# Filter norms: square roots by logarithm, exponential and one Newton step; spectra added up in DRAM

## The chip, the cores and the metric

The kernel runs on one core of a Trainium2 chip. Its parts that matter here are TensorE (matrix products into PSUM), VectorE and GpSimd (elementwise work), ScalarE (elementwise work, and functions looked up in tables that have to be loaded), SyncE (which only issues DMAs here) and 16 DMA engines between on-chip memory (SBUF) and DRAM. Each engine runs its own list of instructions in order, and waits at an instruction until what it needs is there. DMAs are issued from SyncE's queue, from ScalarE's and from GpSimd's; those from GpSimd can add to what stands at the destination. The metric is the device time of one execution, in microseconds.

## The reference

One layer of a hybrid encoder works on a sequence of 1024 steps with 1024 channels: RMS norm, one input projection, a state-space branch (S5), a Hyena branch, a gated merge, an output projection and a final norm. The change touches how the Hyena filters' spectra are made:

```
h = sin(freq * (feats @ w1 + b1));  h = sin(freq * (h @ w2 + b2))
h = (h @ w3) * (exp(-t * |decay|) + 0.05)          # 1024 steps, 2 orders x 2 directions x 1024 channels
k = concat([h_fwd, 0, flip(h_bwd[1:])])            # length 2048
k = k * rsqrt(sum(k * k, axis=0) + 1e-6)           # a norm per channel
kf = rfft(k)                                       # used in both Hyena steps: irfft(rfft(z) * kf)
```

The input's RMS norm, `x * rsqrt(mean(x * x) + 1e-6) * w`, uses the same root function.

## The kernel before

The work goes through stages: the filters (with the input's norm spread among them), then the input projections interleaved with the S5 branch, then the two Hyena convolutions, the branch projections, the merge and the output.

**Filters.** They are made in eight units of 256 channels: two orders times four quarters. `filter_time` makes a unit's filters in eight tiles of 128 time steps. For each tile TensorE multiplies (tile g), ScalarE takes the exponential of the decay (e), VectorE multiplies the two (into e again), ScalarE squares it (sq), and VectorE or GpSimd forms sum and difference of the two directions (so, or ss and sd). For the odd time steps ScalarE and VectorE split these into a high and a low part (sh, sl). GpSimd adds up the squares (acc). `filter_norm` sums acc over the partitions on TensorE (q), takes the root, and corrects one row of the filters with it (transposes into q, then ss). `filter_freq` makes the spectrum: products of the odd time steps (po, 24 matmuls for each of four blocks of frequencies jj) and of the even ones (pe). `join` copies half of pe to SBUF (eo), forms the sum and difference of the even halves (ke), and adds and subtracts po. The four combinations (ko) are stored in the DRAM tensor kspec, one store of 512 KB for each block.

While unit u's time tiles are made, the products of unit u-1 are issued between them; the loop in `filters` sets which step comes with which. A scheduler in the framework then orders each engine's instructions, within the constraints that the code gives (`issue_after`, `high_priority`).

**The root.** `rsqrt` starts from a bit trick and takes three Newton steps, column by column, all on VectorE: for a norm of two columns two operations and twelve small ones, for the input's norm of eight columns two and 48.

**Projections.** Each takes a weight block of 512 KB. `prefetch` loads it (wraw), ScalarE casts it to its high part (whi) and writes the negative of that to wlo, and a DMA from GpSimd's queue adds wraw to wlo. A projection is 48 matmuls; the last 16 read wlo. Three buffers of wraw and two of whi and wlo set how far this runs ahead. `stage_constants` copies the constants of the Hyena stages within DRAM during the first S5 block. kspec is read (tile kt) by `forward`, in the Hyena stages after the S5 branch.

The lines that the steps below name: L119 to L126 the root, L336 the exponential e, L338 its product, L371 the sums q, L383 the transposes, L404 po, L421 eo, L425 and L426 ke, L429 and L430 ko, L508 to L512 the weights' loading, L556 the projections.

Of the kernel before, what the change touches and what calls it, by code (L numbers as in the profile page):

```python
# [9 lines left out]
F = mybir.dt.float32  # L10
# [9 lines left out]
NCH = 256  # L20
# [80 lines left out]
class Trunk:  # L101
# [13 lines left out]
    def rsqrt(self, pool, out, v, n):  # L115

        V = self.nc.vector
        h = pool.tile([128, n], F, name="rsq_h", tag="rsq_h")
        V.tensor_scalar(out=out.bitcast(I32), in0=v.bitcast(I32), scalar1=-0.5, scalar2=float(0x5F3759DF),  # L119
                        op0=ALU.mult, op1=ALU.add)  # L120
        V.tensor_scalar(out=v, in0=v, scalar1=-0.5, scalar2=None, op0=ALU.mult)
        for _ in range(3):
            for c in range(n):
                y, z = out[:, c:c + 1], h[:, c:c + 1]
                V.scalar_tensor_tensor(out=z, in0=y, scalar=v[:, c:c + 1], in1=y, op0=ALU.mult, op1=ALU.mult)  # L125
                V.scalar_tensor_tensor(out=y, in0=z, scalar=1.5, in1=y, op0=ALU.add, op1=ALU.mult)  # L126

# [13 lines left out]
    def setup(self, ctx):  # L141
        tc, nc, I = self.tc, self.nc, self.I
        self.keep = ctx.enter_context(tc.tile_pool(reuse_waits="tile", name="keep", bufs=1))
        self.dram = ctx.enter_context(tc.tile_pool(name="scratch", bufs=1, space=DRAM))
        k = self.keep
        self.ident = k.tile([128, 128], F, name="ident")
        self.ones = k.tile([128, 1], F, name="ones")
        nc.vector.memset(self.ones, 1.0)
        self.par = k.tile([128, 128], F, name="par")
        self.nrm = k.tile([128, 16], F, name="nrm")  # L150
        self.p_norm = self.par[:, 0:8]
        self.p_cw = self.par[:, 8:80].rearrange("p (j c) -> p j c", j=3)
        self.p_cb = self.par[:, 80:104]
        self.p_d = self.par[:, 104:120]
        self.p_bglu = self.par[:, 120:124]
        self.kspec = self.dram.tile([2, 4, 4, 128, 4 * NCH], F, name="kspec")

    def params(self):
# [84 lines left out]
    def filters(self, ctx, top):  # L243
# [13 lines left out]
        for u in range(len(units) + 1):  # L257
# [18 lines left out]
            if u == len(units):  # L276
                self.filter_norm(*units[u - 1], sds)
                c2.close()
                self.weight_pools(top)
                self.proj_pools(top)  # L280
                self.prefetch()
            for i in range(12):
                next(t, None)
                if i == 0 and u < len(units):
                    with tc.high_priority(offset=40):
                        self.filter_norm(*units[u - 1], sds)
                if i >= f0:
                    with tc.issue_after(self.f_g.ins):
                        next(f)
                if i % 3 == 0:  # L290
                    with tc.issue_after(self.f_sq.ins):
                        next(x, None)
                if i == 6 and u + 1 < len(units):
                    self.filter_load(*units[u + 1])()
# [28 lines left out]
    def filter_time(self, o, cq, sds, pool):  # L323
# [6 lines left out]
        for n, tt in enumerate((4, 5, 6, 7, 0, 1, 2, 3)):  # L330
# [32 lines left out]
            yield  # L363

    def filter_norm(self, o, cq, sds):

# [9 lines left out]
        nrm = self.nrm[:, col:col + 2]  # L376
        self.rsqrt(up, nrm, qs, 2)
        r = q[:, NCH:]
        for ct in range(2):
# [8 lines left out]
    def filter_freq(self, o, cq, sds):  # L388
# [7 lines left out]
        def odd(jj):  # L396

            po = pk.tile([128, 2, NCH], F, name="po", bufs=2)
            for part in range(2):
                blocks = (((0, 1, 2, 3), (4, 5, 6, 7)), ((4, 5, 8, 9), (10, 11, 2, 3)))[jj // 2][part]  # L400
                n = 0
                for i, b in enumerate(blocks):
                    for a, d in ((0, 0), (0, 1), (1, 0)):
                        nc.tensor.matmul(out=po[:, part], lhsT=fo[a][:, 12 * (jj % 2) + b], rhs=sd[4 + i][d][:, part],  # L404
                                         start=n == 0 and part == 0, stop=n == 11 and part == 1)
                        n += 1
                yield po

# [8 lines left out]

        def join(j, po):
            pe = even(8 * j + 4, (2, 3))
# [3 lines left out]
            pe = even(8 * j, (0, 1))  # L423
            ke = wp.tile([128, 2, 2, NCH], F, name="ke", bufs=1)
            nc.vector.tensor_tensor(out=ke[:, 0], in0=pe, in1=eo, op=ALU.add)  # L425
            nc.vector.tensor_tensor(out=ke[:, 1], in0=pe, in1=eo, op=ALU.subtract)  # L426
            for jj in (j, j + 2):
                ko = wp.tile([128, 4, NCH], F, name="ko")
                nc.vector.tensor_tensor(out=ko[:, 0:2], in0=ke[:, jj // 2], in1=po[jj], op=ALU.add)  # L429
                nc.vector.tensor_tensor(out=ko[:, 2:4], in0=ke[:, jj // 2], in1=po[jj], op=ALU.subtract)  # L430
                nc.sync.dma_start(out=self.kspec[o, cq, jj], in_=ko.rearrange("p a c -> p (a c)"))

        for j in range(2):
            po = {}
            for jj in (j, j + 2):
                for po[jj] in odd(jj):
                    yield
            yield from join(j, po)
            yield
# [50 lines left out]
    def weight_pools(self, ctx):  # L490
# [8 lines left out]
        self.order += [("w_branch_hy", c, 8) for c in range(8)]  # L499
        self.weights, self.w_more = [], []  # L500

    def prefetch(self):

        nc = self.nc
        while (len(self.weights) < 2 or self.w_more) and self.order:
# [5 lines left out]
            nc.scalar.activation(out=lo, in_=hi, func=AF.Copy, scale=-1.0)  # L511
            nc.gpsimd.dma_start(out=lo, in_=raw, accum_op=ALU.add)  # L512
            self.weights.append((nxt, hi, lo))
# [956 lines left out]
    def run(self):  # L1470
        tc = self.tc
        with ExitStack() as ctx:
# [5 lines left out]
            with ExitStack() as cf:  # L1478
# [3 lines left out]
                with tc.tile_pool(reuse_waits="tile", name="f_mlp", bufs=1, side="right") as mp, \  # L1482
                        tc.tile_pool(reuse_waits="tile", name="f_mlp_ps", bufs=2, space=PSUM, side="right") as mpp:
                    self.filter_mlp(cp, mp, mpp)
                self.filters(cf, ctx)
            self.conv_weights()
            with ExitStack() as c3:
# [52 lines left out]
```

## Time and profile before

Three runs took 1414.94, 1415.73 and 1419.7 us; the median is 1415.73 us. The profiled execution took 1413.96 us, and its span, from the first instruction to the last, is 1412.2 us.

| engine | busy us | share of the span | instructions |
|---|---|---|---|
| TensorE, matmuls | 1346.7 | 95% | 7219 |
| VectorE | 1014.1 | 72% | 1934 |
| ScalarE | 515.1 | 36% | 737 |
| GpSimd | 416.6 | 29% | 343 |

These shares are means over stages with different limits. The page's picture of the span in 40 slices shows VectorE nearly full in the first six (the filters) and TensorE nearly full from the seventh on. A wait is charged to the releaser that came last, and idle time of an engine costs nothing unless something late follows from it. In the rows below, PE is TensorE, PEld its weight loads, DVE VectorE, ACT ScalarE, POOL GpSimd and SP SyncE; a q behind a name is the queue of that engine.

### The profile page before, as it was taken

How to read it: one execution, taken by the hardware profiler on the slowest of the kernel's cores; microseconds unless marked ns; L12 is line 12 of the kernel's file. 1: busy time of each engine (PE TensorE's matmuls, PEld its weight loads, DVE VectorE, ACT ScalarE, POOL GpSimd, SP SyncE). 2: the span in 40 equal slices, each digit the busy share in tenths (PEclk: the TensorE clock that was granted, in tenths of full speed). 3: DMA queues.
4: the chain of work that ended last, by engine and by line, in shares of the span. 5: the costliest groups of instructions: out<-in, count | busy, mean ns of one | idle time of the engine just before them, and what ended most of it. 6: DMA issues, size and time to landing. Idle time of an engine off the chain costs nothing.

```text
span 1412.2 us, 19536 instructions
## 1 busy us (share of the span) xinstructions
PE 1346.7 (95%) x7219; PEld 1135.9 (80%) x7219; DVE 1014.1 (72%) x1934; ACT 515.1 (36%) x737; POOL 416.6 (29%) x343
## 2 busy tenths in 40 slices
PE   5888899999999999999999997999999999999997
PEld 3777798888888887788788885998888889878886
DVE  7999997699599887414479997663899836843632
ACT  5576664222332333333322222443222234422422
POOL 3766675000000000223112213743013223322322
PEclk9999999999999999999999998999999999999999
DMA  8222224865695554566985588769888988755431
GB/s 278 94 78 75 77 100 146 200 173 137 164 301 132 124 124 103 134 173 155 307 244 173 172 241 264 216 179 315 258 268 268 292 247 245 220 161 134 139 112 64
DMA packets 188556, 257.24 MB, mean 182 GB/s; under 512 B 23069, under 2 KB 144153, under 8 KB 185724
## 3 DMA queue, kind: packets, MB, share of 16 engines
q1 hardware_dynamic: 148492, 151.32, 34.0%
q0 software_dynamic: 12608, 43.79, 15.6%
q10 hardware_dynamic: 27360, 60.88, 12.0%
q8 instruction: 57, 0.93, 0.3%
q14 instruction: 39, 0.32, 0.1%
HBM read 147.49 MB, written 76.82 MB: 159 GB/s over the span
## 4 chain that ended last, share of the span: by engine, by line
PE 72%; DVE 18%; DMA 5%; issue 3%; ACT 1%; POOL 1%; SPq 0%; ACTq 0%; DVEq 0%; POOLq 0%
PE pps L556 43%; PE ops L1441 6%; PE iv L643 5%; PE po L404 4%; PE fwo L695 3%; DMA zc<-c_zc_lo_d 2%; PE pe L414 2%; PE pps L536 2%; DVE rsq_h L125 2%; DVE e L338 1%; PE fwe L695 1%; DMA d_y<-x 1%; DVE st L1274 1%; PE zt L680 1%; DVE st L1272 1%
## 5 line engine op out<-in xcount | busy, mean ns | idle before, releaser
L512 POOL DMA_DIRECT2D wlo<-wraw x76 | 66.3, 872 | 673.3 <-ACT wlo L511 530.2
L556 PE MATMUL pps<-xh,whi 128*128 128x512 f32 x848 | 214.2, 400 | 3.2 <-DVE cv L581 3.2
L556 PE MATMUL pps<-xl,whi 128*128 128x512 f32 x848 | 212.3, 397 | 0.0
L556 PE MATMUL pps<-xh,wlo 128*128 128x512 f32 x848 | 210.2, 396 | 0.0
L556 PEld LDWEIGHTS pps<-xh,whi 128*128 128x128 f32 x848 | 158.0, 189 | 39.5 <-ACT wlo L511 3.6
L556 PEld LDWEIGHTS pps<-xh,wlo 128*128 128x128 f32 x848 | 157.9, 188 | 36.8
L556 PEld LDWEIGHTS pps<-xl,whi 128*128 128x128 f32 x848 | 157.3, 188 | 36.3 <-issue 0.2
L510 ACT CAST whi<-wraw 128x1024 fp32r<-128x1024 f32 (+1 forms) x76 | 74.7, 982 | 285.7 <-PE pps L556 254.9
L404 PE MATMUL po<-sh,fo 128*128 128x256 f32 x512 | 101.1, 292 | 6.0 <-DVE sh L111 5.1
L643 PE MATMUL iv<-ic,y 128*128 128x256 f32 (+1 forms) x752 | 97.2, 287 | 5.5 <-POOL y L113 3.1
L643 PEld LDWEIGHTS iv<-ic,y 128*128 128x128 f32 x752 | 95.4, 194 | 8.1 <-POOL y L113 4.0
L404 PEld LDWEIGHTS po<-sh,fo 128*128 128x128 f32 x512 | 84.0, 197 | 8.3 <-DVE sh L111 6.1
L357 POOL TENSOR_TENSOR acc<-acc,sq 128x512 f32<-128x512 f32 x56 | 75.9, 1356 | 24.5 <-ACT sq L342 23.0
L511 ACT ACTIVATE wlo<-whi 128x1024 fp32r<-128x1024 f32 (+1 forms) x76 | 74.9, 985 | 20.7 <-PE pps L556 20.6
L113 DVE TENSOR_TENSOR y<-yraw,y 128x512 fp32r<-128x512 f32 x60 | 55.0, 938 | 28.2 <-ACT y L109 28.2
L404 PE MATMUL po<-sl,fo 128*128 128x256 f32 x256 | 74.2, 290 | 1.0 <-DVE sl L113 1.0
L579 DVE SCALAR_TENSOR_TENSOR cv<-pps,cw,cv 128x1023 f32<-128x1023 f32 x24 | 30.7, 1281 | 59.5 <-ACT cv L578 59.5
L109 ACT CAST y<-yraw 128x512 fp32r<-128x512 f32 x64 | 39.0, 619 | 55.9 <-DMA yraw<-d_y 27.4
L404 PEld LDWEIGHTS po<-sl,fo 128*128 128x128 f32 x256 | 50.4, 197 | 2.2 <-DVE sl L113 1.3
L578 ACT ACTIVATE cv<-pps,cb,cw 128x1024 f32<-128x1024 f32 x24 | 29.0, 1208 | 62.1 <-PE pps L556 43.9
L333 PE MATMUL g<-w3h,ha 128*128 128x512 f32 x64 | 33.3, 520 | 18.6 <-DVE e L338 17.6
L695 PE MATMUL fwo<-z,zc 128*128 128x256 f32 x384 | 49.9, 283 | 0.0
(447 smaller groups left out, 2788.7 us busy)
## 6 DMA issues: line engine op xcount, KB each, us to landing
wlo<-wraw POOLq DMA_DIRECT2D x64, 512.0 KB, 5.7
wraw<-w_in SPq DMA_DIRECT2D x56, 512.0 KB, 5.2
kspec<-ko SPq DMA_DIRECT2D x32, 512.0 KB, 3.6
kt<-kspec SPq DMA_DIRECT2D x32, 512.0 KB, 5.1
yraw<-d_y SPq DMA_DIRECT2D x64, 256.0 KB, 5.3
d_y<-x ACTq DMA_DIRECT2D x28, 512.0 KB, 5.5
d_m<-cv ACTq DMA_DIRECT2D x16, 512.0 KB, 2.6
d_z<-z ACTq DMA_DIRECT2D x8, 1024.0 KB, 5.5
```

What stands on the lines that cost most here:

```text
L109: nc.scalar.copy(out=hi, in_=src)
L113: e.tensor_tensor(out=lo, in0=src, in1=hi, op=ALU.subtract)
L333: nc.tensor.matmul(out=ps, lhsT=ha[:, tsl], rhs=w3h, start=True, stop=False)
L357: nc.gpsimd.tensor_tensor(out=acc, in0=acc, in1=sq, op=ALU.add)
L404: nc.tensor.matmul(out=po[:, part], lhsT=fo[a][:, 12 * (jj % 2) + b], rhs=sd[4 + i][d][:, part], start=n == 0 and part == 0, stop=n == 11 ...
L510: nc.scalar.copy(out=hi, in_=raw)
L511: nc.scalar.activation(out=lo, in_=hi, func=AF.Copy, scale=-1.0)
L512: nc.gpsimd.dma_start(out=lo, in_=raw, accum_op=ALU.add)
L556: self.summed = nc.tensor.matmul(out=ps[:, hf * 512:hf * 512 + 512], lhsT=w[:, kc], rhs=part(x, kc, hf), start=a == 0 and p == 0 and kc == ...
L643: self.rotated = nc.tensor.matmul(out=dst, lhsT=lhsT, rhs=self.ic[b, j][:, cols], start=first, stop=last)
L695: nc.tensor.matmul(out=out, lhsT=zc[a][:, b], rhs=z[:, :, d, zi], start=start and n == 0, stop=stop and n == 3 * len(prods) - 1)
L1441: nc.tensor.matmul(out=pss[cs.start][:, 0:cs.stop - cs.start], lhsT=m[:, kc, ts], rhs=w[kc][:, cs], start=kc == 0 and p == 0, stop=kc == 7 ...
```

## The change

The root becomes a logarithm and an exponential of -0.5 times it on ScalarE, and one Newton step on VectorE for all columns at once. `filter_norm` is cut in two at that point, and its second part is issued three steps later. The products of the odd time steps are no longer added to the even ones on VectorE: ScalarE copies po out of PSUM twice, with both signs, and the result is stored in kspec. The even sums (ke) go to a second DRAM tensor, keven. During the projections, 32 DMAs from GpSimd's queue, two behind each weight's own, add keven to kspec, each row of keven to both halves.

```diff
     def rsqrt(self, pool, out, v, n):
-        V = self.nc.vector
+        nc, V = self.nc, self.nc.vector
         h = pool.tile([128, n], F, name="rsq_h", tag="rsq_h")
-        V.tensor_scalar(out=out.bitcast(I32), in0=v.bitcast(I32), scalar1=-0.5, scalar2=float(0x5F3759DF),
-                        op0=ALU.mult, op1=ALU.add)
+        nc.scalar.activation(out=h, in_=v, func=AF.Ln)
+        nc.scalar.activation(out=out, in_=h, func=AF.Exp, scale=-0.5)
         V.tensor_scalar(out=v, in0=v, scalar1=-0.5, scalar2=None, op0=ALU.mult)
-        for _ in range(3):
-            for c in range(n):
-                y, z = out[:, c:c + 1], h[:, c:c + 1]
-                V.scalar_tensor_tensor(out=z, in0=y, scalar=v[:, c:c + 1], in1=y, op0=ALU.mult, op1=ALU.mult)
-                V.scalar_tensor_tensor(out=y, in0=z, scalar=1.5, in1=y, op0=ALU.add, op1=ALU.mult)
+        V.tensor_tensor(out=h, in0=out, in1=out, op=ALU.mult)
+        V.tensor_tensor(out=h, in0=h, in1=v, op=ALU.mult)
+        V.scalar_tensor_tensor(out=out, in0=h, scalar=1.5, in1=out, op0=ALU.add, op1=ALU.mult)
...
+        self.keven = self.dram.tile([2, 4, 2, 128, 4 * NCH], F, name="keven")
...
                 if i == 0 and u < len(units):
                     with tc.high_priority(offset=40):
-                        self.filter_norm(*units[u - 1], sds)
+                        norm = self.filter_norm(*units[u - 1], sds)
+                        next(norm)
+                if i == 3 and u < len(units):
+                    with tc.high_priority(offset=40):
+                        next(norm, None)
...
+    def filter_sum(self):
+
+        o, cq, jj = self.k_todo.pop(0)
+        ke = self.keven[o, cq, jj % 2][:, 512 * (jj // 2):512 * (jj // 2) + 512]
+        self.nc.gpsimd.dma_start(out=self.kspec[o, cq, jj].rearrange("p (f c) -> p f c", f=2),
+                                 in_=ke.unsqueeze(1).to_broadcast([128, 2, 512]), accum_op=ALU.add)
...
         self.rsqrt(up, nrm, qs, 2)
+        yield
         r = q[:, NCH:]
...
-                yield po
+                if part:
+                    ko = wp.tile([128, 2, 2, NCH], F, name="ko")
+                    for i in range(2):
+                        nc.scalar.activation(out=ko[:, i], in_=po, func=AF.Copy, scale=1.0 - 2 * i)
+                    nc.sync.dma_start(out=self.kspec[o, cq, jj], in_=ko.rearrange("p a b c -> p (a b c)"))
+                yield
...
             pe = even(8 * j, (0, 1))
-            ke = wp.tile([128, 2, 2, NCH], F, name="ke", bufs=1)
+            ke = wp.tile([128, 2, 2, NCH], F, name="ke")
             nc.vector.tensor_tensor(out=ke[:, 0], in0=pe, in1=eo, op=ALU.add)
             nc.vector.tensor_tensor(out=ke[:, 1], in0=pe, in1=eo, op=ALU.subtract)
-            for jj in (j, j + 2):
-                ko = wp.tile([128, 4, NCH], F, name="ko")
-                nc.vector.tensor_tensor(out=ko[:, 0:2], in0=ke[:, jj // 2], in1=po[jj], op=ALU.add)
-                nc.vector.tensor_tensor(out=ko[:, 2:4], in0=ke[:, jj // 2], in1=po[jj], op=ALU.subtract)
-                nc.sync.dma_start(out=self.kspec[o, cq, jj], in_=ko.rearrange("p a c -> p (a c)"))
+            nc.sync.dma_start(out=self.keven[o, cq, j], in_=ke.rearrange("p a b c -> p (a b c)"))
...
-            nc.gpsimd.dma_start(out=lo, in_=raw, accum_op=ALU.add)
+            w_sum = nc.gpsimd.dma_start(out=lo, in_=raw, accum_op=ALU.add)
+            with self.tc.issue_after(w_sum.ins):
+                for _ in self.k_todo[:2]:
+                    self.filter_sum()
...
+            self.k_todo = [(o, cq, jj) for o in range(2) for cq in range(4) for jj in range(4)]
             self.conv_weights()
```

Because a scheduler orders the instructions, three places of the engines' lists are shown. Line numbers after the change are those of the changed kernel. The first place is ScalarE in the middle of the filter stage, where one unit's norm is taken while the next unit's tiles are made. Before, with acc and sq the squares, e the exponential, sh the high part of the odd tiles, xr and xh the input's norm:

```order
L342 ACTIVATE acc<-e 128x512
L342 ACTIVATE sq<-e 128x512 x2
L336 ACTIVATE e<-dec,negt 128x512
L109 CAST sh_1405<-so 128x512
L336 ACTIVATE e<-dec,negt 128x512
```

Now, with rsq_h the logarithm, nrm the root and ko the copies of po:

```order
L346 ACTIVATE acc<-e 128x512
L119 ACT_TABLE_LOAD
L119 ACTIVATE rsq_h<-qs 128x2
L340 ACT_TABLE_LOAD
L340 ACTIVATE e<-dec,negt 128x512
L120 ACTIVATE nrm<-rsq_h 128x2
L422 ACTIVATE ko<-po 128x512
L109 CAST sh_1331<-so 128x512
L422 ACTIVATE ko<-po 128x512
L340 ACTIVATE e<-dec,negt 128x512
```

Two table loads, the logarithm, the exponential for the root and the copies of po now stand between the squares and the exponentials of the next tiles. In the whole list there are 32 table loads; before there were 14.

The second place is ScalarE at the end of the filter stage, where the first projection weights arrive. Before:

```order
L342 ACTIVATE sq<-e 128x512
L479 ACTIVATE xh<-xt,par 128x512
L510 CAST whi<-wraw 128x1024
L511 ACTIVATE wlo<-whi 128x1024
L510 CAST whi<-wraw 128x1024
L511 ACTIVATE wlo<-whi 128x1024
```

Now:

```order
L438 COPY eo<-pe 128x512
L521 CAST whi<-wraw 128x1024
L119 ACT_TABLE_LOAD
L119 ACTIVATE rsq_h<-qs 128x2
L422 ACTIVATE ko<-po 128x512 x2
L522 ACTIVATE wlo<-whi 128x1024
L120 ACT_TABLE_LOAD
L120 ACTIVATE nrm<-rsq_h 128x2
L521 CAST whi<-wraw 128x1024
L422 ACTIVATE ko<-po 128x512 x2
```

The last unit's root and the copies of its first odd products now stand behind the cast of the first weight. On TensorE, 47 rows of the list now stand from those sums (q) to the transposes that need the root; before it was 42.

The third place is GpSimd's list behind the last filter tile. Before:

```order
L362 TENSOR_TENSOR acc<-acc 128x256
L512 DMA wlo<-wraw 128x1024 x24
L822 TENSOR_TENSOR fv<-cv 128x512 x2
```

Now:

```order
L366 TENSOR_TENSOR acc<-acc 128x256
L523 DMA wlo<-wraw 128x1024 x3
L373 DMA kspec<-keven 256x1x512 x2
L523 DMA wlo<-wraw 128x1024
L373 DMA kspec<-keven 256x1x512 x2
```

From the third weight on, two additions into kspec follow each weight's own, for 16 weights.

## Rows read from the trace of the kernel before

**Rows 1.** Stretches: length, busy PE, PEld, DVE, ACT, POOL, PEclk, DMA share, GB/s

```profile
47.00:242.00 195.00, 175.72 (x1099) 155.99 (x1098) 187.09 (x415) 122.90 (x225) 133.99 (x138) 0.96 0.26 94
242.00:260.00 18.00, 18.00 (x110) 16.26 (x110) 7.81 (x24) 4.13 (x5) 1.78 (x2) 1.00 0.86 225
300.00:372.00 72.00, 72.00 (x354) 58.41 (x353) 53.99 (x246) 24.74 (x27) 5.13 (x6) 1.00 0.50 134
380.00:420.00 40.00, 39.49 (x225) 32.60 (x224) 37.82 (x46) 13.31 (x16) 1.70 (x2) 1.00 0.98 302
```

**Rows 2.** Waits from 0 to 262 us: total us, times, longest

```profile
PEld g L333 <- DVE e L338: 23.5, 15, 4.4
```

**Rows 3.** Groups by line, 0 to 262 us: busy us, mean ns, idle before

```profile
L125 DVE SCALAR_TENSOR_TENSOR rsq_h<-nrm,qs 128x1 f32<-128x1 f32 x48 | 21.9, 490 | 0.2
L429 DVE TENSOR_TENSOR ko<-ke,po 128x512 f32<-128x512 f32 x31 | 21.0, 676 | 1.7 <-PE po L404 1.4
L430 DVE TENSOR_TENSOR ko<-ke,po 128x512 f32<-128x512 f32 x30 | 20.3, 675 | 0.0
...
L126 DVE SCALAR_TENSOR_TENSOR nrm<-rsq_h,nrm 128x1 f32<-128x1 f32 x48 | 10.2, 233 | 0.0
...
L125 DVE SCALAR_TENSOR_TENSOR rsq_h<-rs,ssq 128x1 f32<-128x1 f32 x24 | 8.2, 358 | 0.0
...
L126 DVE SCALAR_TENSOR_TENSOR rs<-rsq_h,rs 128x1 f32<-128x1 f32 x24 | 4.4, 196 | 0.0
...
L119 DVE TENSOR_SCALAR nrm<-qs 128x2 int32<-128x2 int32 x8 | 3.1, 384 | 0.1
...
L121 DVE TENSOR_SCALAR qs<-qs 128x2 f32<-128x2 f32 x8 | 2.9, 358 | 0.2
```

**Rows 4.** ScalarE in order of time: start us, us, instruction

```profile
3.92 0.20 ACT L200 ACTIVATE warm<-ones 128x1 f32<-128x1 f32 x1
...
15.65 0.41 ACT L217 ACTIVATE h<-u 64x256 f32<-64x256 f32 x1
16.08 1.28 ACT L336 ACT_TABLE_LOAD   x1
17.38 1.95 ACT L336 ACTIVATE e<-dec,negt 128x512 f32<-128x512 f32 x3
...
80.38 0.56 ACT L421 COPY eo<-pe 128x512 f32<-128x512 f32 x1
80.84 0.62 ACT L457 ACTIVATE xh<-xr 128x512 fp32r<-128x512 f32 x1
```

**Rows 5.** All engines in order of time, end of the filters

```profile
236.93 0.50 PE L371 MATMUL q<-ones,acc 128*128 128x1 f32 x4
...
240.82 1.05 ACT L510 CAST whi<-wraw 128x1024 fp32r<-128x1024 f32 x1 [9.60 <-DMA wraw<-w_in]
...
242.42 0.38 PE L383 MATMUL q<-ident,qs 128*128 128x128 f32 x2
```

**Rows 6.** DMA from 300 to 372 us: queues, an issue with us to landing

```profile
q0 software_dynamic: 864, 3.15, 23.1%
...
q10 hardware_dynamic: 897, 3.28, 11.4%
...
wlo<-wraw POOLq DMA_DIRECT2D x6, 512.0 KB, 4.5
```

**Rows 7.** GpSimd in order of time, the weights' own sums

```profile
272.84 0.84 POOL L512 DMA_DIRECT2D wlo<-wraw  x1 [26.67 <-ACT wlo L511]
...
303.11 0.88 POOL L512 DMA_DIRECT2D wlo<-wraw  x1 [10.36 <-ACT wlo L511]
...
359.11 0.85 POOL L512 DMA_DIRECT2D wlo<-wraw  x1 [10.35 <-ACT wlo L511]
```

**Rows 8.** TensorE in order of time, the matmuls that read wlo

```profile
319.32 3.89 PE L556 MATMUL pps<-xh,wlo 128*128 128x512 f32 x16
```

**Rows 9.** Tile wlo, its DMAs over the whole span

```profile
DMA to landing us min/median/max: 3.2/5.7/19.8
```

More of the change, by code (lines that the diff above doesn't have):

```diff
@@ L276, in filters @@
             if u == len(units):
-                self.filter_norm(*units[u - 1], sds)
+                for _ in self.filter_norm(*units[u - 1], sds):
+                    pass
                 c2.close()
@@ L285, in filters @@
                     with tc.high_priority(offset=40):
-                        self.filter_norm(*units[u - 1], sds)
+                        norm = self.filter_norm(*units[u - 1], sds)
[3 more added lines that the diff above has]
+                        next(norm, None)
                 if i >= f0:
@@ L416, in even, with join @@
             return pe
-        def join(j, po):
+        def join(j):
             pe = even(8 * j + 4, (2, 3))
@@ L423, in join @@
             pe = even(8 * j, (0, 1))
-            ke = wp.tile([128, 2, 2, NCH], F, name="ke", bufs=1)
+            ke = wp.tile([128, 2, 2, NCH], F, name="ke")
             nc.vector.tensor_tensor(out=ke[:, 0], in0=pe, in1=eo, op=ALU.add)
             nc.vector.tensor_tensor(out=ke[:, 1], in0=pe, in1=eo, op=ALU.subtract)
+            nc.sync.dma_start(out=self.keven[o, cq, j], in_=ke.rearrange("p a b c -> p (a b c)"))
+        for j in range(2):
             for jj in (j, j + 2):
-                ko = wp.tile([128, 4, NCH], F, name="ko")
-                nc.vector.tensor_tensor(out=ko[:, 0:2], in0=ke[:, jj // 2], in1=po[jj], op=ALU.add)
-                nc.vector.tensor_tensor(out=ko[:, 2:4], in0=ke[:, jj // 2], in1=po[jj], op=ALU.subtract)
-                nc.sync.dma_start(out=self.kspec[o, cq, jj], in_=ko.rearrange("p a c -> p (a c)"))
-        for j in range(2):
-            po = {}
-            for jj in (j, j + 2):
-                for po[jj] in odd(jj):
-                    yield
-            yield from join(j, po)
+                yield from odd(jj)
+            yield from join(j)
             yield
@@ L499, in weight_pools @@
         self.order += [("w_branch_hy", c, 8) for c in range(8)]
-        self.weights, self.w_more = [], []
+        self.weights, self.w_more, self.k_todo = [], [], []
     def prefetch(self):
```

## Prediction

> **What bounds the kernel now.** I read the busy time by stretches first, since shares over the whole span mix stages. The filter stage fills the first 260 us. In its steady part, 47 to 242 us, VectorE is busy 187.09 of 195 us (96%), TensorE 175.72 (90%), GpSimd 133.99 (69%) and ScalarE 122.90 (63%) [rows 1]. The reader is to see that one engine is full there and that ScalarE has 72 us to spare. The table of waits says the same from the other side: the longest wait of TensorE's weight loads is for VectorE's e, 23.5 us in 15 waits [rows 2]. From 242 us on TensorE is busy 18.00 of 18 and, in the projections, 72.00 of 72 us [rows 1]; what the filters gain comes off the end only if those projections still get their weights in time. So there are three questions: how long the filter stage is, how it hands over to the projections, and whether the new DMA traffic disturbs them.
>
> **What VectorE loses.** Of the 64 additions and subtractions that make ko, 61 fall in the window and take 21.0 + 20.3 = 41.3 us. The eight roots of the norms take 21.9 + 10.2 + 3.1 + 2.9 = 38.1 us, and the Newton steps of the input's norm 8.2 + 4.4 = 12.6 us [rows 3]. Each of the nine roots keeps four small operations; at 0.36 us, the mean of the dearest plain one (L121), that is 12.9 us. VectorE is 41.3 + 38.1 + 12.6 - 12.9 = 79 us lighter and no longer full.
>
> **What ScalarE gets.** 64 copies of po out of PSUM. The nearest row is the copy eo, from the same memory and of the same shape: 0.56 us long, and the next operation starts 0.46 us after it [rows 4]. I take 0.55 (a pair overlaps once), 64 x 0.55 = 35.2 us, with ends of 0.46 and 0.56 (29 to 36 us). Two small activations per root at 0.20 us [rows 4], 18 x 0.20 = 3.6 us. And table loads: the order has 32 where there were 14, because each logarithm and the exponential behind it come from different sets. A load takes 1.28 us; it starts 0.02 us after the operation before it ends, and the next one starts 1.30 us after it [rows 4]. 18 x 1.29 = 23.2 us. In all 62 us.
>
> The Trainium skill, ScalarE: Activation LUTs, section "What ACT_TABLE_LOAD costs", gives about 1.28 us for a load and 1.38 us more for a drain, 2.66 us per switch. This trace agrees on the load and shows no drain; by that rule the 18 loads would cost 48 us instead of 23.
>
> **The steady part.** 56 copies and 8 of the 9 roots fall between 47 and 242 us: 56 x 0.55 + 16 x (1.29 + 0.20) = 30.8 + 23.8 = 54.6 us. ScalarE then has 122.9 + 54.6 = 177.5 us of work, as much as TensorE's 175.7. So the bound does not go away, it moves from VectorE to ScalarE, with TensorE right behind. How long the stretch is depends on how full ScalarE can be kept, in order, between producers on three engines. The rows give two marks in this very stretch: VectorE's 96% when it was the bound and TensorE's 90% as the one next to it. I take the middle, 93%: 177.5 / 0.93 = 191 us, 4 us less than 195. The ends are 185 us (96%) and 202 us (88%, two points under TensorE's mark).
>
> **The hand-over.** Before, the last root ran on VectorE beside everything else: its sums left TensorE at 236.93 us and TensorE transposed the result at 242.42, 5.5 us later, without a stall; ScalarE meanwhile stood 9.60 us, until the first projection weight landed at 240.82 [rows 5]. Now the order puts the logarithm behind that cast on ScalarE, and two copies and a cast between it and the exponential. From the sums on: 3.9 us to the weight, cast 1.05, load and logarithm 1.5, two copies 1.1, another cast of that size 1.05, load and exponential 1.5, then six small VectorE operations, about 1.5: 11.6 us instead of 5.5. Queued behind them are the copies that free po for the last odd products. TensorE has slightly more products between the two points than before (47 instead of 42 rows), which covers some of it. I take 4 us of stall, between 0 (if the weight lands earlier) and 6.
>
> **The new DMAs.** 16 stores of the even sums go out in the filter stage, where the DMA engines are 26% busy [rows 1]: nothing, and little if that cover were gone, since nothing waits for them there. The 32 accumulating DMAs follow 16 weights, two behind each. No row shows such a DMA into DRAM. From below: a plain store of 512 KB costs the 16 engines 11.4% of 72 us for 3.28 MB, or 1.3 us. Nearest: the weights' own accumulation, the same bytes and operation into SBUF, 23.1% of 72 us for six, or 2.77 us [rows 6]. From above: twice that, 5.5 us, if reading the destination in DRAM costs as much again. I take 2.77. A projection lasts 11.2 us (five from 303.11 to 359.11), and the DMA engines are 50% busy then [rows 1, 7]; two sums add 5.5 us: 5.6 + 5.5 = 11.1 of 11.2 us. That just fits. The weight's own sum, issued at 303.11 and landed after 4.5 us, is first read at 319.32 [rows 6 to 8], so it has 11.7 us to spare for waiting behind the two before it in its queue. When the constants are staged (380 to 420 us, 98% busy [rows 1]) a weight's sum already takes up to 19.8 us [rows 9], and TensorE loses only 0.51 us. I take 1 us in all; the ends are 0 and 37 us (third rival). GpSimd has little else to issue there (1.70 of 40 us busy), and nothing is queued behind the new DMAs but the next weight's.
>
> **Sum.** -4 + 4 + 1 = +1 us on the profiled execution's own 1413.96 us. The median of the runs is 1.8 us above that execution, 1415.73: so **1417 us**, no change that can be measured. I count 0.3% (4.2 us) as what a measurement of this kernel can tell from no change.
>
> **Rivals.**
> 1. ScalarE is kept as full as VectorE was. For it: VectorE, now light, answers at once, the roots' second half was given time, and part of the input's scaling can slide into 214 to 242 us, where ScalarE had little to do. Against it: two loads in each root stand in front of the next unit's exponentials. 177.5 / 0.96 = 185, -10; with 2 us at the hand-over, -8: 1408 us.
> 2. ScalarE waits more: each copy stands behind products that TensorE, itself at 90%, delivers late, and blocks the exponentials behind it. It decides from a share of 91%, where 177.5 us need the old 195. At 88%: +7, hand-over +5, DMA +1: 1429 us.
> 3. The DMAs into DRAM cost 5.5 us. Two and the weight's own are 13.8 us per 11.2 us in their queue, and 16.6 with the other queues' share of about 2.8. Nine weights are issued from 272.84 to 359.11 [rows 7], about at this pace; each period adds 5.4 us, 49 in all, of which the slack takes 11.7: TensorE stands up to 37 us. With half of the other queues' work postponed, about +25: 1442 us. For it: no row excludes the price. Against it: the same operation has a row at half of that. It decides from 2.8 us per DMA.
> 4. Each switch of tables costs ScalarE a drain of 1.38 us that the few loads before did not show. 16 loads add 22 us: 199.6 / 0.93 = 215, +20, with the other terms 1441 us. Against it: loads between busy neighbours, as the one at 16.08, show none. That is the page's rule named above.
>
> **How the numbers follow.** Forecast 0.38 (its own range 1410 to 1424), rival 1 0.34, rival 2 0.14, rival 3 0.10, rival 4 0.04. Faster: nearly all of rival 1 and a tenth of the forecast, 0.35. Within 0.3%: two thirds of the forecast and the edges of rivals 1 and 2, 0.28. Slower: the rest of the forecast and rivals 2 to 4, 0.37. The range runs from 1400 (the lower edge of rival 1, with copies at 0.46 us) to 1438 (past rival 2, with about half of rivals 3 and 4 left out).
>
> **What would show it.** In 47 to 242 us (or where that stretch then ends) ScalarE at 91 to 95% and VectorE near 60%, with waits for ScalarE where there were waits for VectorE; loads of 1.28 us with no gap before or behind; the last pair of transposes about 10 us after their sums with TensorE idle before them; accumulating DMAs with a share of some 2.8 us each and TensorE still full from 300 to 372 us. The forecast is wrong if ScalarE's share is above 95% or under 90%, or if the projections show waits for weights.

## The result, and the profile after

The changed kernel takes 1440.18 us, the median of four runs (1432.71 to 1442.36); the kernel before, on the same chip, 1415.77 (1414.94 to 1419.70). The ratio is 1.0155, with a 95% interval from 1.0119 to 1.0192: slower by 1.5%. I forecast 1417 us and gave "slower" no more than 0.37; the time lies 2 us above the top of my range (the ratio times the 1415.73 us that I started from is 1437.7, just under it). The profiled execution took 1438.68 us, its span 1436.9.

Read in the order of the prediction, the stretches come first (columns as in [rows 1]; kernel after):

```profile
47.00:242.00 195.00, 173.98 (x1112) 155.63 (x1111) 126.16 (x226) 172.40 (x314) 136.37 (x140) 0.98 0.37 132
242.00:260.00 18.00, 18.00 (x105) 15.97 (x104) 8.36 (x39) 7.58 (x13) 1.78 (x2) 1.00 0.99 271
300.00:372.00 72.00, 71.35 (x349) 57.30 (x348) 50.40 (x222) 24.98 (x28) 18.32 (x18) 1.00 1.06 242
372.00:420.00 48.00, 41.31 (x205) 34.08 (x203) 39.29 (x58) 10.54 (x15) 9.19 (x9) 0.93 1.07 269
420.00:510.00 90.00, 79.69 (x486) 66.71 (x485) 65.06 (x98) 23.78 (x30) 12.22 (x12) 0.92 0.87 197
```

Against [rows 1] the reader is to see two things. In the filter stage VectorE falls from 187.09 to 126.16 us and ScalarE rises from 122.90 to 172.40, and yet the stage is as long as it was. And from 300 to 420 us the DMA share, the last but one column, is above 1. It adds up the time of all packets as a share of the 16 engines' time, so it can pass 1; before it was 0.50 to 372 us and 0.92 to 420. From 300 to 372 us TensorE stays nearly full all the same, 71.35 of 72 us; after that it doesn't: 6 us are missing to 420 us, and 10 of 90 from 420 to 510, at a granted clock of 0.92.

The filter stage in detail. The first fence is the waits up to 262 us (answering [rows 2]), the second the groups by line (answering [rows 3]), the third ScalarE in order of time at one root (answering [rows 4]), all of the kernel after:

```profile
PEld g L337 <- DVE e L342: 29.4, 20, 4.4
...
DVE qs L121 <- ACT rsq_h L119: 16.1, 7, 4.4
```

```profile
L422 ACT ACTIVATE ko<-po 128x512 f32<-128x512 f32 x64 | 34.3, 589 | 5.4 <-PE po L416 5.4
...
L119 ACT ACT_TABLE_LOAD x9 | 11.5, 1283 | 0.2
...
L340 ACT ACT_TABLE_LOAD x8 | 10.3, 1283 | 0.1
```

```profile
160.25 0.60 ACT L109 CAST sh<-so 128x512 fp32r<-128x512 f32 x1
160.87 1.28 ACT L119 ACT_TABLE_LOAD   x1
162.16 0.20 ACT L119 ACTIVATE rsq_h<-qs 128x2 f32<-128x2 f32 x1
162.27 0.67 ACT L490 ACTIVATE xh<-xt,par 128x512 fp32r<-128x512 f32 x1
162.96 1.28 ACT L340 ACT_TABLE_LOAD   x1
```

The copies cost 34.3 us where I took 35.2, and a load stands 0.02 us behind a cast and 0.01 us ahead of the logarithm: no drain. The wait of TensorE's weight loads for e did not go with VectorE's work, it grew from 23.5 us [rows 2] to 29.4.

The end of the filters, all engines in order of time (answering [rows 5]):

```profile
236.69 0.50 PE L382 MATMUL q<-ones,acc 128*128 128x1 f32 x4
...
237.61 1.05 ACT L521 CAST whi<-wraw 128x1024 fp32r<-128x1024 f32 x1 [2.99 <-DMA wraw<-w_in]
...
244.51 0.45 PE L395 MATMUL q<-ident,qs 128*128 128x128 f32 x2
```

The sums leave TensorE at 236.69 us, 0.24 earlier than before [rows 5], and the transposes follow after 7.8 us (5.5 before, 11.6 forecast), because the weight landed 3.2 us earlier. TensorE stays busy 18.00 of the next 18 us. So at 242 us nothing is lost and nothing won. All of it is lost later, and the rows point at the DMA engines. The first fence is the queues and issues of 310 to 400 us (answering [rows 6]), the second ScalarE in order of time:

```profile
q0 software_dynamic: 5257, 12.12, 73.5%
...
kspec<-keven POOLq DMA_DIRECT2D x16, 512.0 KB, 14.5
...
wlo<-wraw POOLq DMA_DIRECT2D x8, 512.0 KB, 9.4
```

```profile
391.06 1.06 ACT L1165 COPY ntr<-s5ps 128x512 f32<-128x512 f32 x2
406.50 0.33 ACTq L762 DMA_DIRECT2D d_m<-cv  x1
406.87 1.07 ACT L1165 COPY nti<-s5ps 128x512 f32<-128x512 f32 x2 [14.74 <-DMA m<-ts]
...
447.57 0.36 ACTq L762 DMA_DIRECT2D d_m<-cv  x1
447.98 1.05 ACT L1240 COPY t<-s5ps 32x512 f32<-32x512 f32 x2 [16.89 <-DMA d_y<-y]
```

In these 90 us GpSimd's queue takes 73.5% of 16 engines, 66.2 us; less eight weights at 2.77 [rows 6] that leaves 44.0 us for sixteen sums, 2.75 each (an estimate, since the weights' own price is taken from the kernel before). A weight's sum lands after 9.4 us instead of 4.5. The second fence shows what that does: ScalarE stands 14.74 and 16.89 us ahead of a store of 512 KB (d_m<-cv), and the profile names late 64 KB transfers of the S5 stage as what released it. The store reads none of their data. Why it waits for them the trace does not show. Behind the store, in order, stand the copies that TensorE's next S5 products need. The waits from 372 to 510 us (the first five rows are left out, four for other engines and one of GpSimd for a DMA):

```profile
...
ACT t L1240 <- DMA d_y<-y: 16.9, 1, 16.9
ACT nti L1165 <- DMA m<-ts: 14.7, 1, 14.7
PEld s5ps L1163 <- issue: 10.9, 2, 6.9
DVE st L1284 <- DMA d_y<-y: 10.4, 1, 10.4
ACT ntr L1165 <- DMA ts<-t: 9.7, 1, 9.7
DVE ni L1180 <- DMA ts<-t: 9.1, 2, 7.6
```

In the same view of the kernel before no row is for a DMA. The raw weights, too, took 18.7 us from issue to landing between 380 and 510 us (median; 5.2 before). The chain of work that ended last runs through four DMAs here, 65 of the 73 us from 374.82 to 447.50 us:

```profile
374.82 17.78 DMA ts<-t
...
394.77 10.73 DMA m<-ts
...
406.69 23.17 DMA c_ic_d<-c_ic
...
433.80 13.70 DMA d_y<-y
```

The first, second and fourth are small S5 transfers (56 and 64 KB), the third is part of the copy of the constants. In the kernel before the chain runs through TensorE and VectorE there.

The next table follows the lag through the kernel: the time in the span at which GpSimd issues a weight's own sum, less the time in the kernel before (us, from the instructions in order of time; the runs e1 to e12 are those of the next section).

| before at | after | e1 | e2 | e3 | e6 | e7 | e9 | e10 | e12 |
|---|---|---|---|---|---|---|---|---|---|
| 243 | -0.9 | 0.4 | -2.2 | 0.0 | 34.1 | 4.4 | -1.3 | -1.3 | 14.9 |
| 292 | -1.2 | 0.6 | -2.5 | 0.2 | 35.3 | 5.7 | -0.8 | -0.2 | 12.7 |
| 359 | 8.6 | 0.6 | -2.5 | 0.2 | 35.3 | 14.0 | -0.8 | -0.2 | 12.7 |
| 391 | 0.0 | 0.6 | -2.5 | 0.3 | 35.3 | 5.7 | -0.8 | -0.2 | 12.8 |
| 422 | 9.5 | 0.6 | -2.5 | 0.3 | 35.3 | 15.0 | -0.8 | -0.2 | 12.8 |
| 473 | 23.4 | 0.6 | 2.4 | 6.1 | 35.3 | 16.7 | -0.8 | 10.7 | 13.9 |
| 677 | 23.5 | 0.3 | 3.2 | 14.6 | 36.5 | 20.8 | 5.0 | 11.8 | 13.5 |
| 814 | 23.0 | 0.4 | 3.1 | 14.2 | 36.4 | 20.7 | 7.8 | 10.6 | 13.5 |
| 826 | 23.0 | 0.4 | 3.1 | 14.2 | 36.4 | 20.7 | 19.9 | 10.6 | 13.5 |
| 970 | 24.9 | 2.5 | 3.1 | 16.4 | 38.3 | 21.2 | 36.2 | 10.9 | 14.6 |
| 1294 | 25.4 | 3.1 | 4.0 | 17.3 | 38.9 | 22.4 | 36.7 | 11.6 | 17.4 |

A single issue can be late for a moment: the 8.6 us at 359 are gone at 391. So up to 391 us the sums cost nothing that lasts, with the engines' share at 1.06. The changed kernel's lag comes between 391 and 473 us, where the S5 blocks' small transfers and the copy of the constants run beside the sums, and it stays.

### The profile page after: what moved, and what is told of

It reads as the page before. It is cut to its first block, busy times and chain, and to the rows that moved or that the text cites. A ratio compares the mean times of both kernels' runs of the same rounds, so it can differ in the third digit from the quotient of the medians.

```text
span 1436.9 us, 19533 instructions
## 1 busy us (share of the span) xinstructions
PE 1353.5 (94%) x7219; PEld 1143.4 (80%) x7219; DVE 950.0 (66%) x1744; ACT 567.7 (40%) x837; POOL 444.1 (31%) x375
## 3 DMA queue, kind: packets, MB, share of 16 engines
q1 hardware_dynamic: 150796, 159.71, 35.2%
q10 hardware_dynamic: 27360, 60.88, 11.8%
## 4 chain that ended last, share of the span: by engine, by line
PE 64%; DMA 15%; DVE 10%; ACT 6%; issue 3%; SPq 1%; ACTq 1%; POOL 0%; DVEq 0%; POOLq 0%
PE pps L570 37%; PE ops L1455 6%; PE iv L657 5%; PE fwo L709 3%; PE po L416 3%; DMA zc<-c_zc_lo_d 2%; DMA ts<-t 2%; PE pe L431 2%; PE pps L550 2%; DMA wraw<-w_in 2%; DMA wlo<-wraw 2%; DMA c_ic_d<-c_ic 2%; PE fwe L709 2%; DVE st L1288 1%; DMA d_y<-y 1%
## 5 line engine op out<-in xcount | busy, mean ns | idle before, releaser
L570 PEld LDWEIGHTS pps<-xh,wlo 128*128 128x128 f32 x848 | 159.4, 190 | 38.3 <-DMA wlo<-wraw 1.0
L416 PE MATMUL po<-sh,fo 128*128 128x256 f32 x512 | 105.4, 293 | 5.9 <-DVE sh L111 5.9
L657 PEld LDWEIGHTS iv<-ic,y 128*128 128x128 f32 x752 | 99.3, 202 | 4.4 <-DVE y L113 2.1
L657 PE MATMUL iv<-ic,y 128*128 128x256 f32 (+1 forms) x752 | 100.4, 294 | 2.5 <-DVE y L113 1.8
L109 ACT CAST y<-yraw 128x512 fp32r<-128x512 f32 x64 | 38.9, 619 | 59.8 <-PE iv L657 31.5
L342 DVE SCALAR_TENSOR_TENSOR e<-e,g 128x512 f32<-128x512 f32 x64 | 43.1, 679 | 21.5 <-ACT e L340 10.9
L337 PE MATMUL g<-w3h,ha 128*128 128x512 f32 x64 | 32.7, 511 | 23.3 <-DVE e L342 22.2
```

Source lines behind the costliest of these rows:

```text
L109: nc.scalar.copy(out=hi, in_=src)
L342: nc.vector.scalar_tensor_tensor(out=h, in0=e, scalar=0.05, in1=ps, op0=ALU.add, op1=ALU.mult)
L570: self.summed = nc.tensor.matmul(out=ps[:, hf * 512:hf * 512 + 512], lhsT=w[:, kc], rhs=part(x, kc, hf), start=a == 0 and p == 0 and kc == ...
L657: self.rotated = nc.tensor.matmul(out=dst, lhsT=lhsT, rhs=self.ic[b, j][:, cols], start=first, stop=last)
```

## The experiments

Theory T: the 32 sums' bytes fill the 16 DMA engines; the small transfers of the S5 blocks and the raw weights land late, and TensorE stands. Rival U: not the bytes, but GpSimd's issues and their place ahead of the next weight's sum. Rival V: the filter stage, where ScalarE is now the fullest engine, costs the time. Rival W: the collision with the copy of the constants at 370 to 420 us. Each run was timed beside runs of the kernel before, whose medians lay between 1415.98 and 1418.08 us; the ratios are to those, with 95% intervals.

**e1: no sums.**

```
-            self.k_todo = [(o, cq, jj) for o in range(2) for cq in range(4) for jj in range(4)]
```

> Leaves out the 32 sums (the even-time sums are not added into the stored spectra). Theory T (the bytes of the sums fill the 16 DMA engines between 280 and 440 us; the S5 stage's small transfers and the raw weights land late, and TensorE stands): 1413 to 1418 us, the whole of the +24 gone, share of the DMA queues in 300 to 372 back from 1.06 to about 0.5. Theory U (not the bytes, but GpSimd's issues and their place ahead of the next weight's own sum): the same here. Theory V (the filter stage, where ScalarE is now 88% busy, costs the time and is paid for later): 1432 to 1440 us.

Measured: 1415.38 us, ratio 0.9989 (0.9975 to 1.0003). The whole loss hangs on the sums, and V is out. What is left of the change, with all of its work in the filter stage, makes no difference that can be measured. The stretches of e1, as above:

```profile
47.00:242.00 195.00, 175.85 (x1103) 157.83 (x1102) 125.75 (x226) 170.76 (x312) 135.38 (x139) 0.96 0.36 129
...
300.00:372.00 72.00, 72.00 (x351) 58.27 (x350) 51.03 (x227) 24.20 (x26) 5.12 (x6) 1.00 0.52 139
```

**e2: short rows.** The same 32 DMAs with as many rows, each 64 columns long instead of 512.

```
-        ke = ...[:, 512 * (jj // 2):512 * (jj // 2) + 512]
+        ke = ...[:, 512 * (jj // 2):512 * (jj // 2) + 64]
-        dma_start(out=self.kspec[o, cq, jj].rearrange(...), in_=ke...to_broadcast([128, 2, 512]), ...)
+        dma_start(out=self.kspec[o, cq, jj].rearrange(...)[:, :, 0:64], in_=ke...to_broadcast([128, 2, 64]), ...)
```

> All 32 sums are issued at their places and with as many rows, but each row is an eighth as long (64 of 512 columns; the rest is not added). T: most of the +24 goes, 1414 to 1422 us, since the queue of the sums takes a third or less of the time that it took. U: 1432 to 1440, since GpSimd issues the same number of rows at the same places. V: 1432 to 1440.

Measured: 1417.10 us, ratio 0.9996 (0.9983 to 1.0008). GpSimd issues as much, at the same places, and nothing that can be measured is lost (the table has 5 us between 422 and 473, made up for by a filter stage 2.5 us shorter in the execution profiled). So U is out for these places, but for those 5 us at most; what the long rows cost the DMA engines remains. The share from 300 to 372 us is 0.70.

**e3: one sum behind each weight.**

```
-                for _ in self.k_todo[:2]:
+                for _ in self.k_todo[:1]:
```

> One sum behind each weight instead of two, so the 32 sums stretch over twice as many weights, half of them beyond the S5 blocks. T: the DMA engines' share between 300 and 440 falls to about 0.8 and the lag shrinks by more than half: 1417 to 1428 us. U: the number of issues is the same, 1432 to 1440. V: 1432 to 1440.

Measured: 1429.66 us, ratio 1.0088 (1.0055 to 1.0121), a little above what T expected. The table shows two steps of the lag, 6 us between 422 and 473, while the S5 blocks run, and 8 us between 473 and 677. The stretches where they fall:

```profile
420.00:510.00 90.00, 84.57 (x508) 69.66 (x504) 75.53 (x124) 26.39 (x33) 9.90 (x11) 1.00 0.79 172
...
600.00:700.00 100.00, 95.03 (x408) 75.82 (x407) 31.06 (x22) 33.43 (x42) 33.66 (x27) 0.98 0.98 233
```

The second is beyond the S5 blocks, with the engines at 0.98 (0.73 before). The first, at a mean of 0.79, says that a stretch can lose time before its mean share reaches 1.

**e7: the constants copied earlier**, in the filter stage.

```
+                if u == 4 and i == 9:
+                    self.stage_constants()
...
-                    if gb == 0:
-                        with tc.issue_after(self.s5_loaded.ins):
-                            self.stage_constants()
```

> The changed kernel, both sums behind each weight, but the 7 MB of constants are copied to DRAM in the filter stage (unit 4) instead of at 370 to 420 us. T: the engines are still full from 300 to 372 us (share 1.06), the part of the lag that arose after 400 us (9 to 23 us) shrinks: 1424 to 1434 us. W (the collision of the sums with that copy is the whole of it): 1414 to 1419 us. If neither counts: 1436 to 1442 us.

Measured: 1434.39 us, ratio 1.0127 (1.0100 to 1.0154). W is out as the whole cause, but it has a part. The copy costs about 5 us in the filter stage (4.4 for -0.9 at 243 us), and what comes after 292 us shrinks from 26.6 to 16.7 us: some 10 us hang on the sums and the copy running at the same time. From 300 to 372 us the share is 1.07 as in the changed kernel.

**e10: overwrite in place of add.**

```
-                                 in_=ke.unsqueeze(1).to_broadcast([128, 2, 512]), accum_op=ALU.add)
+                                 in_=ke.unsqueeze(1).to_broadcast([128, 2, 512]))
```

> The 32 transfers keep their places, their rows and their 512 KB each, but overwrite the stored rows in place of adding to them (the odd-time products are lost). T: a row that is only written takes the engines about half of what a row that is added takes (by the two kinds of rows of this trace, 1.4 in place of 2.75 us for 512 KB), the share in 300 to 372 us falls from 1.06 to about 0.8, and most of the lag goes: 1417 to 1427 us. If the bytes count and not the time that the adding takes: 1432 to 1440 us.

Measured: 1425.07 us, ratio 1.0063 (1.0046 to 1.0081), inside T's range; the share from 300 to 372 us is 0.92, where T had about 0.8. The queue, 300 to 372 us:

```profile
q0 software_dynamic: 2675, 9.71, 53.6%
...
kspec<-keven POOLq DMA_DIRECT2D x12, 512.0 KB, 8.3
...
wlo<-wraw POOLq DMA_DIRECT2D x7, 512.0 KB, 5.6
```

38.6 us less seven weights at 2.77 leaves 19.2 us for twelve, 1.6 each against 2.75 with the addition. The number of transfers and their 512 KB are the same, all queues together move more in these 72 us (18.31 MB against 17.40 in the changed kernel), and yet more than half of the lag is gone. So it is the time on the engines that counts, not the bytes as such. One thing changed beside the adding: the queue's rows come to about 140 packets for an overwriting transfer and about 260 for an adding one. That the number of packets alone does the harm is ruled out by e2, whose sums have as many rows and cost nothing measurable.

**e9: later**, one sum behind each weight from the end of the S5 blocks on. Here I sharpened T: only the S5 blocks' small transfers make the sums dear.

```
+            self.k_todo = [...]       # moved behind the S5 blocks
             with ExitStack() as c4:
...
+                for _ in self.k_todo[:1]:
```

> The changed kernel with the 32 sums moved behind the S5 blocks, one behind each weight from about 500 us to 860 us. T, sharpened: the sums' bytes turn into lost time because the S5 blocks' 64 KB transfers and the stores that wait behind them land late; beyond the S5 blocks there are none, and the engines' share there, 0.6 to 0.7, rises to about 0.9 only: 1416 to 1426 us. Rival: the engines' time is short everywhere, and the sums cost as much at any place as one behind each weight from the start did (0.9%): 1428 to 1440 us.

Measured: 1450.43 us, ratio 1.0250 (1.0219 to 1.0280), worse than both places above. The sharpened theory fell. Stretches of e9:

```profile
640.00:700.00 60.00, 54.14 (x229) 42.63 (x227) 26.05 (x17) 15.79 (x22) 21.13 (x18) 0.97 1.06 249
700.00:760.00 60.00, 54.44 (x261) 45.04 (x261) 26.14 (x31) 16.64 (x20) 15.58 (x12) 0.94 0.99 254
...
880.00:900.00 20.00, 6.45 (x37) 5.74 (x37) 19.13 (x23) 2.18 (x4) 8.38 (x7) 0.59 1.05 313
```

From 640 to 760 us the raw weights of the branches, the gates (cv<-d_m) and a table of constants (zc) land late, with the engines full. Yet the table has a lag of only 7.8 us left at 814; the larger part, some 28 us, comes between there and 970. In the last row TensorE is busy 6.45 of 20 us while VectorE is at 19.13, at a granted clock of 0.59, a mean of time at 1.2 and at 2.4 GHz. What makes that larger part I did not test. The last sums are issued at 882 and 933 us, long after the first read of kspec (714 us); a read that waits for its sum would be a rival, but the chain that ended last has no such read from 805 to 935 us.

**e6: earlier**, 28 sums one unit behind their stores, inside the filter stage, the last four after it.

```
+                if u > 1 and i in (1, 4, 7, 10):
+                    with tc.issue_after(self.f_g.ins):
+                        self.filter_sum()
```

> The changed kernel with 28 of the 32 sums issued one unit after their stores, inside the filter stage, and 4 behind the first two weights after it. T: the DMA engines have room there (share 0.37 of 195 us, 28 times 2.75 us raises it to some 0.77), GpSimd has 58 us idle and takes about 31 for the issues: 1414 to 1422 us. Rival: GpSimd's accumulations and odd sums run late, TensorE waits in the filter stage, and the time only moves: 1428 to 1440 us.

Measured: 1451.39 us, ratio 1.0242 (1.0217 to 1.0266). T's number was wrong by some 30 us; the rival named there came in, and beyond. Of the lag of 39 us 34 are there at 243 us. GpSimd's longest wait ahead of a sum, from 47 to 242 us, is for the even sums' stores (keven<-ke):

```profile
POOL kspec L377 <- DMA keven<-ke: 22.2, 4, 9.1
```

GpSimd in order of time (a sum and what stood behind it; "issue" is idle time for which the profile shows no releaser):

```profile
104.67 0.74 POOL L370 TENSOR_TENSOR acc<-acc 128x256 f32<-128x256 f32 x1
112.28 2.11 POOL L377 DMA_DIRECT2D kspec<-keven  x2 [6.86 <-issue]
113.43 1.71 POOL L357 TENSOR_TENSOR so<-e 128x256 f32<-128x256 f32 x1
```

**e12: e6 with e2's short rows**, to part GpSimd's queue from the bytes.

```
+                if u > 1 and i in (1, 4, 7, 10):   # and the rest of e6
...
+        ... in_=ke.unsqueeze(1).to_broadcast([128, 2, 64]), ...   # and the rest of e2
```

> The run with the sums in the filter stage (2.4% slower than the kernel before), with each row an eighth as long (64 of 512 columns; the rest is not added). If the bytes did it there too (the engines' share was 0.70 of 195 us, with stretches of 20 us at 0.83 to 0.93, and the even sums' stores took up to 10 us to land): 1415 to 1424 us. If GpSimd's queue did it (each sum waits there for its stores to land, with the odd sums that TensorE needs behind it, and an issue takes 1.1 us): 1436 to 1452 us.

Measured: 1429.58 us, ratio 1.0084 (1.0056 to 1.0112), between the two. Of the 2.4% about a third stays with short rows (13 to 15 us of lag at 243 to 292); I put it down to GpSimd's queue, by elimination. The rest goes with the long rows. The two are not apart, though: with short rows GpSimd waits 1.4 us for those stores where it waited 22.2 in e6.

**e4: the new root alone**, in the kernel before, with the norm's second half three steps later; **e11**: that delay alone, with the old root; **e5**: e1 with the old root.

```
     def rsqrt(...):            # e4 and e11: the kernel before; e5: the changed kernel without sums
+        nc.scalar.activation(out=h, in_=v, func=AF.Ln)                        # e4 only
+        nc.scalar.activation(out=out, in_=h, func=AF.Exp, scale=-0.5)         # e4 only
...
         self.rsqrt(up, nrm, qs, 2)
+        yield                  # e4 and e11
```

> The kernel before with nothing changed but the root (logarithm, exponential, one Newton step, and the norm's second half three steps later). T: the roots' table loads lie in ScalarE's idle time of a filter stage that DVE holds at 187 of 195 us, DVE gets about 4 us less work: 1409 to 1416 us. V: ScalarE's loads and the waits of TensorE for the exponentials cost time already here: 1420 us or more.

> The kernel before with the second half of each unit's norm three steps later and nothing else. If the later half is what the run with only the root paid for (0.6%): 1421 to 1427 us. If the root paid it, by VectorE's wait for two table loads, a logarithm and an exponential in the middle of a filled stage: 1413 to 1418 us.

> The changed kernel without the 32 sums (even-time sums not added) and with the old root on VectorE, so that of the change the signed copies on ScalarE, the separate stores and the later second half of the norm are left. If the root costs in the changed filter stage what it cost alone (the kernel with nothing but the root took 0.6% more than the kernel before), the copies give some 6 us back: 1405 to 1412 us. If with ScalarE at 171 of 195 us the stage goes by other waits and the root makes no difference there: 1413 to 1418 us.

Measured: e4 1426.14 us, ratio 1.0061 (1.0039 to 1.0083); e11 1420.14, 1.0013 (0.9996 to 1.0029); e5 1417.71, 1.0006 (0.9994 to 1.0019). Alone, the new root costs 0.6%, and of the delay nothing can be measured; in the company of the copies the root costs nothing, and the copies win nothing. T's number for e4 was wrong and V's came in, but not V's reason: TensorE's wait for e from 47 to 242 us is 15.9 us, and 16.7 in the kernel before. What e4 does show is that VectorE loses work (160.61 us where it had 187.09) and gains waits for the root in the middle of its queue. That these waits are the price is argued, not shown: the changed kernel has more of them (16.1 us for the logarithm) and e1 doesn't pay. The filter stage of e4 and of e5, and what VectorE waits for in e4 from 47 to 250 us:

```profile
47.00:242.00 195.00, 170.22 (x1049) 150.36 (x1048) 160.61 (x278) 146.80 (x257) 133.14 (x138) 0.95 0.23 84
```

```profile
47.00:242.00 195.00, 171.59 (x1081) 154.14 (x1080) 156.16 (x347) 146.02 (x275) 135.93 (x140) 0.96 0.34 125
```

```profile
DVE qs L121 <- ACT rsq_h L119: 8.7, 5, 3.0
...
DVE rsq_h L122 <- ACT nrm L120: 5.7, 5, 1.5
```

In e5 no engine but TensorE is above 81%, and the stage is as long, within 3 us, as with VectorE at 96% or ScalarE at 88%.

**e8: e6 with the old root** on VectorE.

```
+                if u > 1 and i in (1, 4, 7, 10):   # and the rest of e6
...
-        nc.scalar.activation(out=h, in_=v, func=AF.Ln)
-        nc.scalar.activation(out=out, in_=h, func=AF.Exp, scale=-0.5)
+        V.tensor_scalar(out=out.bitcast(I32), ...)   # and three Newton steps, as before; in e5 too
```

> As the run with the sums in the filter stage, with the old root on VectorE. Two effects that add: 6 to 8 us below that run if the root costs in this stage, 1406 to 1416 us; the same as that run within 2 us if it doesn't.

Measured: 1448.43 us, ratio 1.0227 (1.0208 to 1.0245), 3 us under e6: neither the 6 to 8 nor the 2 us expected, and within both intervals, so the root's part in this stage can't be told. The sums rule. No complete version with the sums reaches the kernel before (the nearest, e3, is 0.9% slower), and without them the change is worth nothing measurable; a version that beats both was not found.

## Why the prediction was wrong

**The sum of three terms.** I had -4 for the steady part, +4 for the hand-over and +1 for the DMAs. e1 measures the first two together: 0.9989, about -1.6 us, and within its interval none. Their sum, 0, was right by luck: the lag at 243 us is -0.9 in the changed kernel and 0.4 in e1, so neither the -4 nor the +4 is there. The DMA term is the difference between the changed kernel and e1: 1.0155 less 0.9989 is 0.0166 of 1416, 23.5 us. That is the term that failed.

**The step that failed** is not the price of a sum: 2.77 us taken, 2.75 measured, and rival 3's condition "cost 5.5 us" did not hold. Yet its result, about +25, came in almost to the microsecond; that is luck, since it came another way. The step is "that just fits": I set two sums against one projection of 11.2 us at the share of 300 to 372 us, 0.50. In that stretch it did fit: TensorE is busy 71.35 of 72 us, and the lag at 391 us is 0.0. But sixteen weights with two sums each do not end at 372; the last are issued at 497. In the kernel before the DMA share, by the same view, went on so:

```profile
260.00:300.00 40.00, 39.96 (x178) 31.92 (x177) 32.61 (x247) 11.18 (x12) 2.53 (x3) 1.00 0.84 197
...
372.00:420.00 48.00, 47.49 (x285) 39.99 (x284) 45.53 (x64) 14.46 (x18) 2.55 (x3) 1.00 0.92 277
420.00:510.00 90.00, 89.95 (x529) 74.62 (x526) 81.14 (x127) 27.22 (x35) 5.10 (x6) 1.00 0.57 133
```

Room from 260 to 510 us: 40 x 0.16 + 72 x 0.50 + 48 x 0.08 + 90 x 0.43 = 6.4 + 36.0 + 3.8 + 38.7 = 84.9 us. The sums need 32 x 2.75 = 88 us. By this estimate they did not fit even on average. Fitting on average would not have been enough either: e10's cheaper transfers need only 32 x 1.6 = 51 us, and it still lags by 11.6 us. The second half of the same step failed with it: I asked only how long the weight's own sum could wait (11.7 us of slack), and not who else waits on those engines. e1, e2 and e10 show that the loss follows the engines' time (shares of 0.52, 0.70, 0.92 and 1.06 from 300 to 372 us, in e1, e2, e10 and the changed kernel, go with ratios of 0.9989, 0.9996, 1.0063 and 1.0155).

The Trainium skill, DMA: Bandwidth & Descriptors, section "Issuing engines are not separate DMA queues", says that transfers issued by ScalarE, SyncE and GpSimd run on the same 16 engines and interleave. The trace agrees: with GpSimd's sums at 73.5% of the engines' time, SyncE's S5 transfers landed late and ScalarE's store stood 14.74 and 16.89 us. I had counted only what was queued behind the sums on GpSimd.

**The steady part.** Wrong by the 4 us, and wrong in reason. "The bound moves from VectorE to ScalarE" would have the length follow the fullest engine. ScalarE's 177.5 us of work came out at 172.4, its share at 88%, the mark that I gave to rival 2 and under the 90% that I had named as a sign of being wrong; but the stretch did not get 7 us longer. e5, with no engine but TensorE above 81%, is as long again. So the length does not follow the fullest of the other engines. Whether VectorE's 96% in [rows 1] set it before, these runs can't tell, since all that relieve VectorE load ScalarE. TensorE keeps 87 to 90% of the stage in the kernel before, the changed one, e1, e4 and e5, with a wait for e in each; what would shorten the stage I did not find.

**The hand-over.** The chain through ScalarE is there as written, but it begins 3.2 us earlier, since the raw weight landed at 237.61 instead of 240.82 us: 7.8 us, covered whole by TensorE's other products. My lower end, 0, was right.

**The rivals.** Rival 1 (96%): no, 88%. Rival 2: its share came, its time didn't. Rival 4: loads stand between their neighbours with gaps of 0.01 to 0.02 us. The drain of the Trainium skill, ScalarE: Activation LUTs, "What ACT_TABLE_LOAD costs", does not appear, as the prediction had it. The Trainium skill, ScalarE: Activation LUTs, "Table sets: the hidden batching unit", gives a logarithm followed by an exponential one load, from a set that has both; this kernel has two per root, 18 in nine.

## What to carry to other kernels

Add up the engines' time that new DMAs need and the room in every stretch in which they will run, not in the stretch where they start; and list all who use those engines there, small transfers in a dependent chain above all, not only the queue that issues them. Room on average is a first test, not a pass. An engine at 96% is a bound only if relieving it moves the end: moving 61 us off VectorE, and 50 onto ScalarE, moved nothing here. Two parts of a change need not add up: the new root cost 8 us alone and nothing beside the copies.

## What the runs showed of the hardware that was not expected

- Adding 512 KB into DRAM by DMA took the 16 engines 2.75 us, overwriting them from GpSimd with the same access, in about half as many packets, 1.6 us (both worked out from the queue's share).
- With the engines' share at 1.06 from 300 to 372 us TensorE lost 0.65 us; at 1.07 and 0.87 in the next two stretches, where the S5 blocks' small transfers run, it lost 6 and 10 us against the kernel before.
- With the engines full, a store stood in ScalarE's in-order queue for 14.74 and 16.89 us until 64 KB transfers that it does not read had landed.
- The granted clock fell with the stalls: 0.92 from 420 to 510 us (part of it at 1.2 GHz) where it was 1.00 before, 0.59 in the 20 us of e9 in which TensorE was busy 6.45.
